# Weight rows 1088 bytes apart and activations in a high and a low block, in a two-layer encoder

## The chip, the cores and the metric

The kernel runs on one core of one Trainium2 chip. The metric is the time of one execution on the device in microseconds; less is better. A median of three runs is given for the kernel before.

## The reference

A two-layer encoder over 256 tokens and 16 learned meta tokens (272 rows), width 2048, all in float32. Each layer does this:

```python
h = rmsnorm(x)
q, k, v, f, ga, gf = split(h @ w_in)              # one input projection
attn = softmax(rope(norm(q)) @ rope(norm(k)).T / sqrt(128)) @ v   # 8 heads, 2 key/value heads
fr   = Re(fft2(f))                                # per group of 128 channels, over positions and channels
x = x + (sigmoid(ga) * (attn @ w_attn_br) + sigmoid(gf) * (fr @ w_four)) @ w_out
h2 = rmsnorm(x)
x = x + (silu(dwconv3(h2 @ w_up_gate)) * (h2 @ w_up_val)) @ w_down    # inner width 5632
```

The 16 meta rows are put in front before layer 0 and dropped at the end.

## The kernel before

Activations lie transposed in SBUF: channels over the 128 partitions, tokens along the free dimension. A projection takes a tile of 128 x 128 weights as the stationary operand and a tile of activations, 128 channels by all tokens, as the moving one.

To keep float32 accuracy with the `float32r` type, every operand is split into a high part and a low part, and a product is three matmuls: high weights by high activations, high weights by low activations, low weights by high activations (L357, L358, L359 in `group`). Where two tokens' halves fit one PSUM bank, the first two are one matmul of twice the width (L353).

Weights stream from HBM in chunks of 512 KB: 4 row tiles (`CW`) of 128 rows by 256 columns (`MG` = 2 column tiles). The list `order` holds all groups of chunks in the order in which they are used, and `chunks` is that list flattened. `load_raw` (L238) issues the transfer of a chunk into a ring of 4 buffers `raw`, and in some stages every third chunk into one of 2 more buffers `raw5`. `advance` (L254) keeps the transfers that far ahead of TensorE and puts splits on the list `todo`. `split_w` (L279) makes the high part `wh` on ScalarE (L286) and the low part `wl` on VectorE (L288), each in a ring of 3 buffers of 128 x 4 x 256 elements. `next_split` hands a pair to `group`. `fold_w` makes sums and differences of weight rows for the Fourier groups of layer 0 in the buffer `wpm`.

The normalised input of a layer's projections is `xHL`: for each of the 16 channel tiles the high part of 272 tokens and behind it the low part, so a tile takes 2176 bytes of a partition. `gHL` (inner activations of layer 0) has the same form. The high and low parts of the query and attention tiles (`q`, tags q1 and q2) and of the gated merge (`mH`, `mL`, in the tiles aH and aL) are separate tiles with 1088 bytes for each channel tile.

Layer 0 works on all 272 tokens. Layer 1 leaves the first 14 out in most projections (258 columns) and all 16 in the value half of its feed-forward part (2 x 256 columns).

The order of a layer: the Fourier inputs (`f`), `k`, `v`, `q`; then the mixing stage, two halves of the branch groups `ga`, `gf`, `s`, `a` in the order BRANCH_ORDER, each half followed by 8 groups `o` of the output projection; then the feed-forward part. In layer 0 this is `ug` and `uv` for 24 and then 20 inner tiles, each followed by 8 groups `d`. In layer 1 a fast scheme of block products is mixed in: `products` (L1402) multiplies activations by weights with the roles exchanged, so that the 128 x 128 activation tile (`opnd`, or a part of `xHL`) is stationary and 512 columns of weights move (L1419). At the end four groups `t` (tails, L1500) do the same for the inner tiles that are left. The generator `prepare` makes the sums of weights which these products need, on VectorE and with GpSimd's queue for its transfers, while layer 0's feed-forward part runs. Small work (attention, norms, Fourier steps) sits in generators in the list `shadow`, and `step` runs one piece of it after every second triple of matmuls.

TensorE's instructions run in program order. SBUF tiles come from pools: `per` (whole run), `wp` (weight buffers), and one pool for each stage, `mix0`, `ffn0`, `mix1`, `ffn1`.

Of the kernel before, what the change touches and what calls it, by code (L numbers as in the profile page):

```python
# [10 lines left out]
F32 = mybir.dt.float32  # L11
F32R = mybir.dt.float32r
# [4 lines left out]
P = 128  # L17
# [43 lines left out]
TAIL_ORDER = (2, 3, 0, 1)  # L61
F0 = 1536

def _branch(text):
# [91 lines left out]
def encoder_kernel(ctx, tc, xT, params, consts, bmat, cfold, csign, w_fl, w_f64c, w_in, w_abr, w_four, w_f64, w_out, w_up, w_down, w_vn, w_dn, w_dt, out):  # L156
# [53 lines left out]

    chunks, folded, mix, summed, stage, small_w = [], set(), {}, {}, {}, {}
    t, done = 0, 0
    for key, chs in order:
        for j, ch in enumerate(chs):
            n = 0
            if key[0] == 1 and key[1] in ("t", "ug", "uv"):
                n = due(t) - done
                t += 1
            if n:
                mix[key, j] = n  # L220
                for s, p, k in PRODUCTS[done:done + n]:
                    if p in (3, 4, 5, 6):
                        summed[len(chunks)] = (min(s, len(VSETS)), (3, 0, 1, 2)[p - 3], k)
                    chunks.append(pchunks[done])
                    done += 1
                first_mix = min(first_mix, len(chunks) - n) if done > n else len(chunks) - n
            if key[:2] == (0, "s"):
                folded.add(len(chunks))
            if key[1] in BRANCH:
                stage[len(chunks)] = key[0]  # L230
                if key[1] == "gf" and j == 0:
                    small_w[len(chunks) + KT // CW] = (key[0], key[2])
            chunks.append(ch)
    st = {"raw": 0, "fetch": 0, "next": 0, "grp": 0, "stage": None}
    raws, splits = {}, {}
    RAW, LOOK = 4, 2

    def load_raw(i):  # L238
        src, n = chunks[i]
        assert i not in summed or summed[i] in ready_sums  # L240
        if i in small_w:
            assert "r64" not in st
            st["r64"] = wp.tile([64, MG * P], F32, tag="r64", name="r64", bufs=1)
            nc.sync.dma_start(st["r64"], w_f64[small_w[i]])
        if (i >= first_mix if st["stage"] == DEPTH else stage.get(i, -1) == st["stage"]) and (i - first_mix) % 3 == 2:
            r = st["pool"].tile([P, CW, MG * P], F32, tag="raw5", name=f"raw{i}", bufs=2)
        else:
            r = wp.tile([P, CW, MG * P], F32, tag="raw", name=f"raw{i}", bufs=RAW)
        nc.sync.dma_start(r, src)
        raws[i] = r  # L250
# [3 lines left out]
    def advance(upto):  # L254
        while st["raw"] < min(upto + RAW + 2 * (upto > first_mix or stage.get(upto, -1) == st["stage"]), len(chunks)):
# [17 lines left out]
    def fold_w(i):  # L273
        r = wp.tile([P, CW, MG * P], F32, tag="wpm", name=f"wpm{i}", bufs=1)
        for o, op in ((0, ALU.add), (2, ALU.subtract)):
            nc.vector.tensor_tensor(r[:, o:o + 2], raws[i][:, 0:2], raws[i][:, 2:4], op=op)
        raws[i] = r

    def split_w(i, a, b, parts="hl"):  # L279
        if i not in splits:  # L280
            splits[i] = tuple(wp.tile([P, CW, MG * P], F32R, tag=t, name=f"{t}{i}") for t in ("wh", "wl"))
        h, lo = splits[i]
# [82 lines left out]
    def split_w64(l, i):  # L365
        r = st.pop("r64")
        w = wp.tile([96, MG * P], F32R, tag="w64", name="w64", bufs=2)
# [70 lines left out]
    XT = per.tile([P, KT, T], F32, name="XT")  # L438
    xf = per.tile([P, KT * 2 * T + 8], F32R, name="xHL")
    xHL = xf[:, :KT * 2 * T].rearrange("p (k r t) -> p k r t", k=KT, r=2)  # L440
    xH, xL = xHL[:, :, 0, :], xHL[:, :, 1, :]
    prm = per.tile([P, P_N], F32, name="prm")
# [57 lines left out]
    def norm_split(m, goff):  # L500
        gc = prm[:, goff + m:goff + m + 1]
        nc.scalar.activation(xH[:, m, :], XT[:, m, :], AF.Copy, scale=gc)
        nc.vector.scalar_tensor_tensor(xL[:, m, :], XT[:, m, :], gc, xH[:, m, :].bitcast(F32),
# [109 lines left out]
    for l in range(DEPTH):  # L613
        last = l == DEPTH - 1
        lo = 14 if last else 0
        lo2 = 16 if last else 0
        W, W2 = T - lo, T - lo2
        hold = {}

        with tc.tile_pool(name=f"mix{l}", bufs=1) as mp:  # L620
            E = mp.tile([P, 4, 2, TH] if last else [P, NG, T], F32, tag="q1b" if last else "q1", name="E")
            e64 = mp.tile([2 * NG, TH], F32, tag="u", name="e64", bufs=2) if last else None
            AHn = 3 * 4 * T
            ALn = 2 * 4 * T
            o1 = []
# [425 lines left out]
            def attention(kv, rq):  # L1051
# [8 lines left out]
                PH = PHf.rearrange("p (b h t) -> p b h t", b=3, h=4)  # L1060
                PL = PLf.rearrange("p (b h t) -> p b h t", b=2, h=4)

# [89 lines left out]
            for i in range(4):  # L1152
# [3 lines left out]
                if last:  # L1156
                    if i in (0, 2):
                        until(hold, "vt" if i == 0 else "fold")
                        for t_, n in ((qH, "q1"), (qL, "q2")):
                            t_.append(mp.tile([P, 4, T], F32R, tag=n + "ab"[i // 2], name=n))  # L1160
                elif i == 0:
                    until(hold, "vt")
                    until(hold, "fold")
                    for t_, n in ((qH, "q1"), (qL, "q2")):
                        t = mp.tile([P, NH, T], F32R, tag=n, name=n)
                        t_ += [t[:, 0:4], t[:, 4:8]]
# [25 lines left out]
            for half in range(2):  # L1192
                mH = mL = None
                for n_, (kind, i) in enumerate(BRANCH_ORDER[half]):
# [45 lines left out]
        with tc.tile_pool(name=f"ffn{l}", bufs=1) as fp:  # L1240
# [50 lines left out]
            if last:  # L1291
                X0, X1 = 26, 32
                XF = XT.rearrange("p k t -> p (k t)")
                asum = XF[:, 0:NQ * P].rearrange("p (k t) -> p k t", k=NQ)
                own = fp.tile([P, KS - (X1 - X0), SEQ], F32, name="act")
                lent = XF[:, NQ * P:NQ * P + (X1 - X0) * SEQ].rearrange("p (k t) -> p k t", t=SEQ)
# [145 lines left out]
                for i in UP_ORDER:  # L1442
# [136 lines left out]
```

## Time and profile before

| | us |
|---|---|
| median of 3 runs | 2527.54 (2526.27 to 2527.87) |
| the profiled execution | 2529.31 |
| its span in the profile | 2527.5 |
| TensorE busy (PE) | 2517.7 |
| weight loads busy (PEld) | 2436.3 |
| VectorE busy (DVE) | 1987.5 |
| ScalarE busy (ACT) | 1340.5 |
| GpSimd busy (POOL) | 203.9 |

The profile is of one execution. A matmul's duration in it is that of a pipelined instruction, which overlaps the next; how fast TensorE goes is read from the distance between starts, or from the count of matmuls in a stretch. PEld rows are weight loads: each matmul has one, and it runs beside the matmul before it. A row of the windows gives, for a stretch, each engine's busy time and its instruction count in brackets, the granted clock of TensorE (1.00 is full), the busy share of the DMA engines and what they moved in GB/s. Rows of the timeline give start, length, engine, line, operation and operands, written as output<-inputs; neighbours of one kind are merged and counted.

### The profile page before, as it was taken

To read this page: it belongs to the slowest core of one execution; us is meant where nothing else is said; L and a number is where in the kernel's file an instruction comes from. 1 tells how busy PE (TensorE), PEld (TensorE's weight loads), DVE (VectorE), ACT (ScalarE), POOL (GpSimd) and SP (SyncE) were. 2 spreads that over 40 slices of the span, in tenths; PEclk is the share of its full clock that TensorE was granted. 3 is DMA by queue.
4 is the path that set the end of the run, shared out by engine and by line. 5 is a ranking of instruction groups with operands and counts; after the bars stand their busy time and mean duration, and the time that the engine had idled before them with its cause. 6 is when DMAs were issued, how large, how long until landed. Compare 5 with 4: busy or idle time off the path is not lost.

```text
span 2527.5 us, 47924 instructions
## 1 busy us (share of the span) xinstructions
PE 2517.7 (100%) x18848; PEld 2436.3 (96%) x18848; DVE 1987.5 (79%) x3159; ACT 1340.5 (53%) x1913; POOL 203.9 (8%) x394
## 2 busy tenths in 40 slices
PE   9999999999999999999999999999999999999999
PEld 8999999999999999999999999999988899998887
DVE  7687866778878667888768877666878787898898
ACT  5455444554444334444445555444676665666665
POOL 0000000012212221222200000000000000000000
PEclk9999999999999999999999999999999999999999
DMA  7544558879999999999975647888888887788887
GB/s 248 167 155 157 190 190 249 260 247 371 394 324 387 391 378 380 378 383 386 390 280 195 201 154 232 270 256 261 255 262 290 299 290 236 261 280 288 279 302 269
DMA packets 194802, 706.85 MB, mean 280 GB/s; under 512 B 22144, under 2 KB 27392, under 8 KB 194320
## 3 DMA queue, kind: packets, MB, share of 16 engines
q1 hardware_dynamic: 146768, 517.09, 58.6%
q0 software_dynamic: 46368, 184.57, 21.2%
q8 instruction: 147, 2.41, 0.4%
q10 hardware_dynamic: 1440, 2.13, 0.2%
q14 instruction: 79, 0.65, 0.1%
HBM read 623.32 MB, written 111.15 MB: 291 GB/s over the span
## 4 chain that ended last, share of the span: by engine, by line
PE 99%; DVE 0%; DMA 0%; issue 0%; POOL 0%; ACT 0%; ACTq 0%; POOLq 0%
PE ps_p L1419 14%; PE ps_ug L359 7%; PE ps_ug L358 7%; PE ps_ug L357 7%; PE ps_d L358 4%; PE ps_uv L358 4%; PE ps_d L357 3%; PE ps_uv L359 3%; PE ps_d L359 3%; PE ps_uv L357 3%; PE ps_o L358 2%; PE ps_ga L358 2%; PE ps_gf L358 2%; PE ps_o L357 2%; PE ps_ga L359 2%; PE ps_o L359 2%
## 5 line engine op out<-in xcount | busy, mean ns | idle before, releaser
L286 ACT CAST wh<-raw 128x1024 fp32r<-128x1024 f32 (+1 forms) x961 | 999.9, 1045 | 913.4 <-PE ps_ug L358 214.5
L288 DVE TENSOR_TENSOR wl<-raw,wh 128x1024 fp32r<-128x1024 f32 (+1 forms) x961 | 1158.4, 1216 | 410.2 <-ACT wh L286 399.3
L358 PE MATMUL ps_ug<-xHL,wh 128*128 128x272 f32 (+1 forms) x1408 | 401.5, 285 | 0.0
L357 PE MATMUL ps_ug<-xHL,wh 128*128 128x272 f32 (+1 forms) x1408 | 400.8, 285 | 0.0
L359 PE MATMUL ps_ug<-xHL,wl 128*128 128x272 f32 (+1 forms) x1408 | 400.5, 286 | 0.1
L358 PEld LDWEIGHTS ps_ug<-xHL,wh 128*128 128x128 f32 x1408 | 264.7, 188 | 3.2
L357 PEld LDWEIGHTS ps_ug<-xHL,wh 128*128 128x128 f32 x1408 | 264.6, 188 | 3.3
L359 PEld LDWEIGHTS ps_ug<-xHL,wl 128*128 128x128 f32 x1408 | 264.1, 188 | 1.2 <-DVE wl L288 0.8
L1419 PE MATMUL ps_p<-wh,opnd 128*128 128x512 f32 x816 | 222.7, 393 | 0.0
L358 PE MATMUL ps_uv<-xHL,wh 128*128 128x272 f32 x704 | 203.3, 289 | 0.0
L358 PE MATMUL ps_d<-gHL,wh 128*128 128x272 f32 x704 | 202.9, 288 | 0.0
L357 PE MATMUL ps_d<-gHL,wh 128*128 128x272 f32 x704 | 202.9, 288 | 0.0
L359 PE MATMUL ps_uv<-xHL,wl 128*128 128x272 f32 x704 | 202.6, 288 | 0.0
L357 PE MATMUL ps_uv<-xHL,wh 128*128 128x272 f32 x704 | 202.3, 287 | 0.0
L359 PE MATMUL ps_d<-gHL,wl 128*128 128x272 f32 x704 | 202.1, 287 | 0.0
L1419 PEld LDWEIGHTS ps_p<-wh,opnd 128*128 128x128 f32 x816 | 148.4, 188 | 29.4 <-ACT wh L286 0.2
L357 PE MATMUL ps_ga<-xHL,wh 128*128 128x272 f32 (+1 forms) x512 | 147.8, 289 | 0.0
L519 DVE TENSOR_TENSOR wi<-wi,wi 128x512 f32<-128x512 f32 x224 | 146.8, 684 | 0.0
L357 PE MATMUL ps_gf<-xHL,wh 128*128 128x272 f32 (+1 forms) x512 | 146.8, 287 | 0.0
L358 PE MATMUL ps_o<-mL,wh 128*128 128x272 f32 (+1 forms) x512 | 146.5, 286 | 0.0
L358 PE MATMUL ps_ga<-xHL,wh 128*128 128x272 f32 (+1 forms) x512 | 146.1, 285 | 0.0
L359 PE MATMUL ps_o<-mH,wl 128*128 128x272 f32 (+1 forms) x512 | 146.1, 285 | 0.0
(380 smaller groups left out, 5969.4 us busy)
## 6 DMA issues: line engine op xcount, KB each, us to landing
raw<-in_w_up SPq DMA_DIRECT2D x288, 512.0 KB, 6.3
raw<-in_w_in SPq DMA_DIRECT2D x191, 512.0 KB, 3.8
raw<-in_w_down SPq DMA_DIRECT2D x88, 512.0 KB, 7.0
wi<-in_w_dn POOLq DMA_DIRECT2D x80, 512.0 KB, 9.7
ft<-wi POOLq DMA_DIRECT2D x80, 512.0 KB, 7.9
raw<-ft SPq DMA_DIRECT2D x80, 512.0 KB, 4.6
raw<-in_w_out SPq DMA_DIRECT2D x64, 512.0 KB, 4.2
raw<-fv SPq DMA_DIRECT2D x64, 512.0 KB, 4.8
```

What stands on the lines that cost most here:

```text
L286: nc.scalar.copy(h[:, a:b], r[:, a:b])
L288: nc.vector.tensor_tensor(lo[:, a:b], r[:, a:b], h[:, a:b].bitcast(F32), op=ALU.subtract)
L357: nc.tensor.matmul(o, h[:, c, sl], a, start=kt == 0, stop=False)
L358: nc.tensor.matmul(o, h[:, c, sl], b, start=False, stop=False)
L359: nc.tensor.matmul(o, lo[:, c, sl], a, start=False, stop=kt == nk - 1)
L519: tt = lambda *v, **kw: tc.keep_in_program_order(nc.vector.tensor_tensor(*v, **kw))
L1419: nc.tensor.matmul(ps[h], x, w[:, 512 * h:512 * h + 512], start=fresh and (s_, q) in BEGIN and first, stop=(s_, q) in END and end, skip_gr ...
```

## The change

The split weights `wh` and `wl` become flat buffers of 4 x 272 elements; a row tile's 256 columns take the first 256 of each 272, so row tiles lie 1088 bytes apart, as far as the activation tiles of 272 tokens. Chunks that serve as the moving operand (the products and the tails, the set `streamed`) stay dense, 1024 bytes apart, in the same buffers. `xHL` and `gHL` are laid out as one block of all high parts and one of all low parts. The starts of `xHL` (one for each layer), `gHL`, the query tiles, `mH`, `mL` and `opnd` are moved by fixed numbers of elements, and `act` gets 48 unused elements behind it, which moves what lies behind. To make room, the small weight buffers `r64`, `w64` and `wpm` go from the pool `wp` to the stage's pool, and in layer 0's mixing stage one extra buffer `raw5` is kept instead of two, so the transfers run five chunks ahead there instead of six.

```diff
+CS = T
+X_PAD, X_AT = 64, (28, 60)
+G_AT = 12
+M_AT = ((60, 60), (22, 22))
+Q_AT = (((12,), (20,)), ((62, 46), (62, 62)))
+A_PAD, O_AT = 48, 16
...
+                    streamed.add(len(chunks))
                     chunks.append(pchunks[done])
...
+            if key[:2] == (1, "t"):
+                streamed.add(len(chunks))
...
+    def extra(i):
+        if st["stage"] == DEPTH:
+            return 2 * (i >= first_mix)
+        return 0 if st["stage"] is None or stage.get(i, -1) != st["stage"] else 1 + st["stage"]
...
-        if (i >= first_mix if st["stage"] == DEPTH else stage.get(i, -1) == st["stage"]) and (i - first_mix) % 3 == 2:
-            r = st["pool"].tile([P, CW, MG * P], F32, tag="raw5", name=f"raw{i}", bufs=2)
+        more = extra(i)
+        if more and (i - first_mix) % (2 + 3 // more) == 1 + 3 // more:
+            r = st["pool"].tile([P, CW, MG * P], F32, tag="raw5", name=f"raw{i}", bufs=more)
...
+    def weight_rows(w, dense):
+        if dense:
+            return w[:, :CW * MG * P].rearrange("p (c m) -> p c m", c=CW)
+        return w.rearrange("p (c m) -> p c m", c=CW)[:, :, :MG * P]
...
-            splits[i] = tuple(wp.tile([P, CW, MG * P], F32R, tag=t, name=f"{t}{i}") for t in ("wh", "wl"))
+            splits[i] = tuple(weight_rows(wp.tile([P, CW * CS], F32R, tag=t, name=f"{t}{i}"), i in streamed) for t in ("wh", "wl"))
...
-    xf = per.tile([P, KT * 2 * T + 8], F32R, name="xHL")
-    xHL = xf[:, :KT * 2 * T].rearrange("p (k r t) -> p k r t", k=KT, r=2)
-    xH, xL = xHL[:, :, 0, :], xHL[:, :, 1, :]
+    xf = per.tile([P, KT * 2 * T + X_PAD], F32R, name="xHL")
+    xHLs = [xf[:, o:o + KT * 2 * T].rearrange("p (r k t) -> p r k t", r=2, k=KT) for o in X_AT]
+    xHL, xH, xL = xHLs[0], xHLs[0][:, 0], xHLs[0][:, 1]
...
-            ALn = 2 * 4 * T
+            ALn = 2 * 4 * T + M_AT[l][1]
...
-                            t_.append(mp.tile([P, 4, T], F32R, tag=n + "ab"[i // 2], name=n))
+                            o = Q_AT[l][t_ is qL][i // 2]
+                            t = mp.tile([P, 4 * T + o], F32R, tag=n + "ab"[i // 2], name=n)
+                            t_.append(t[:, o:o + 4 * T].rearrange("p (h t) -> p h t", t=T))
...
-                            mH = mHf[:, :8 * T].rearrange("p (k t) -> p k t", k=8)
-                            mL = mLf[:, :8 * T].rearrange("p (k t) -> p k t", k=8)
+                            mH = mHf[:, M_AT[l][0]:M_AT[l][0] + 8 * T].rearrange("p (k t) -> p k t", k=8)
+                            mL = mLf[:, M_AT[l][1]:M_AT[l][1] + 8 * T].rearrange("p (k t) -> p k t", k=8)
...
-                gHL = fp.tile([P, FF_SPLIT[0], 2, T], F32R, tag="gHL", name="gHL")
-                gH, gL = gHL[:, :, 0, :], gHL[:, :, 1, :]
+                gf = fp.tile([P, FF_SPLIT[0] * 2 * T + G_AT], F32R, tag="gHL", name="gHL")
+                gH, gL = (gf[:, G_AT + FF_SPLIT[0] * T * r:G_AT + FF_SPLIT[0] * T * (r + 1)].rearrange("p (k t) -> p k t", t=T) for r in range(2))
...
-                own = fp.tile([P, KS - (X1 - X0), SEQ], F32, name="act")
+                own = fp.tile([P, (KS - (X1 - X0)) * SEQ + A_PAD], F32, name="act")
...
-                    t_ = fp.tile([P, 2, 3, P], F32R, tag="opnd", name="opnd", bufs=2)
+                    t_ = fp.tile([P, 6 * P + 64], F32R, tag="opnd", name="opnd", bufs=2)
+                    t_ = t_[:, O_AT:O_AT + 6 * P].rearrange("p (r n t) -> p r n t", r=2, n=3)
...
-                        ps = group((l, "uv", i), lambda kt: (xHL[:, kt, :, lo2:T],), W2)
+                        ps = group((l, "uv", i), lambda kt: (xHL[:, :, kt, lo2:T],), W2)
```

More of the change, by code (lines that the diff above doesn't have):

```diff
@@ L209, in due @@
         return d0 + (d1 - d0) * (t - t0) // (t1 - t0)
-    chunks, folded, mix, summed, stage, small_w = [], set(), {}, {}, {}, {}
+    chunks, folded, streamed, mix, summed, stage, small_w = [], set(), set(), {}, {}, {}, {}
     t, done = 0, 0
@@ L242, in load_raw @@
             assert "r64" not in st
-            st["r64"] = wp.tile([64, MG * P], F32, tag="r64", name="r64", bufs=1)
+            st["r64"] = st["pool"].tile([64, MG * P], F32, tag="r64", name="r64", bufs=1)
             nc.sync.dma_start(st["r64"], w_f64[small_w[i]])
-        if (i >= first_mix if st["stage"] == DEPTH else stage.get(i, -1) == st["stage"]) and (i - first_mix) % 3 == 2:
-            r = st["pool"].tile([P, CW, MG * P], F32, tag="raw5", name=f"raw{i}", bufs=2)
+        more = extra(i)
+        if more and (i - first_mix) % (2 + 3 // more) == 1 + 3 // more:
+            r = st["pool"].tile([P, CW, MG * P], F32, tag="raw5", name=f"raw{i}", bufs=more)
         else:
@@ L254, in advance @@
     def advance(upto):
-        while st["raw"] < min(upto + RAW + 2 * (upto > first_mix or stage.get(upto, -1) == st["stage"]), len(chunks)):
+        while st["raw"] < min(upto + RAW + extra(upto), len(chunks)):
             load_raw(st["raw"])
@@ L273, in fold_w @@
     def fold_w(i):
-        r = wp.tile([P, CW, MG * P], F32, tag="wpm", name=f"wpm{i}", bufs=1)
+        r = st["pool"].tile([P, CW, MG * P], F32, tag="wpm", name=f"wpm{i}", bufs=1)
         for o, op in ((0, ALU.add), (2, ALU.subtract)):
@@ L366, in split_w64 @@
         r = st.pop("r64")
-        w = wp.tile([96, MG * P], F32R, tag="w64", name="w64", bufs=2)
+        w = st["pool"].tile([96, MG * P], F32R, tag="w64", name="w64", bufs=2)
         nc.scalar.copy(w[0:64], r)
@@ L501, in norm_split @@
         gc = prm[:, goff + m:goff + m + 1]
+        xH, xL = (xHLs[goff // KT % DEPTH][:, r] for r in range(2))
         nc.scalar.activation(xH[:, m, :], XT[:, m, :], AF.Copy, scale=gc)
@@ L617, in encoder_kernel @@
         W, W2 = T - lo, T - lo2
+        xHL, xH, xL = xHLs[l], xHLs[l][:, 0], xHLs[l][:, 1]
         hold = {}
@@ L1060, in attention @@
                 PH = PHf.rearrange("p (b h t) -> p b h t", b=3, h=4)
-                PL = PLf.rearrange("p (b h t) -> p b h t", b=2, h=4)
+                PL = PLf[:, :2 * 4 * T].rearrange("p (b h t) -> p b h t", b=2, h=4)
                 def scores(item):
@@ L1164, in encoder_kernel @@
                     for t_, n in ((qH, "q1"), (qL, "q2")):
-                        t = mp.tile([P, NH, T], F32R, tag=n, name=n)
+                        o = Q_AT[l][t_ is qL][0]
+                        t = mp.tile([P, NH * T + o], F32R, tag=n, name=n)[:, o:o + NH * T].rearrange("p (h t) -> p h t", t=T)
                         t_ += [t[:, 0:4], t[:, 4:8]]
@@ L1294, in encoder_kernel @@
                 asum = XF[:, 0:NQ * P].rearrange("p (k t) -> p k t", k=NQ)
-                own = fp.tile([P, KS - (X1 - X0), SEQ], F32, name="act")
+                own = fp.tile([P, (KS - (X1 - X0)) * SEQ + A_PAD], F32, name="act")
+                own = own[:, :(KS - (X1 - X0)) * SEQ].rearrange("p (k t) -> p k t", t=SEQ)
                 lent = XF[:, NQ * P:NQ * P + (X1 - X0) * SEQ].rearrange("p (k t) -> p k t", t=SEQ)
```

## The prediction

> **What bounds the kernel now.** I read the page's busy times and its chain first, then the groups, then the windows, then the timeline of TensorE.
>
> ```profile
> span 2527.5 us, 47924 instructions
> PE 2517.7 (100%) x18848; PEld 2436.3 (96%) x18848; DVE 1987.5 (79%) x3159; ACT 1340.5 (53%) x1913; POOL 203.9 (8%) x394
> PE 99%; DVE 0%; DMA 0%; issue 0%; POOL 0%; ACT 0%; ACTq 0%; POOLq 0%
> L286 ACT CAST wh<-raw 128x1024 fp32r<-128x1024 f32 (+1 forms) x961 | 999.9, 1045 | 913.4 <-PE ps_ug L358 214.5
> L288 DVE TENSOR_TENSOR wl<-raw,wh 128x1024 fp32r<-128x1024 f32 (+1 forms) x961 | 1158.4, 1216 | 410.2 <-ACT wh L286 399.3
> L358 PE MATMUL ps_ug<-xHL,wh 128*128 128x272 f32 (+1 forms) x1408 | 401.5, 285 | 0.0
> ```
>
> TensorE never waits: the chain is 99% matmuls, and L358 has 0.0 us of idle time before 1408 of them. ScalarE, which makes the high part of every weight (L286), idles 913 us, most of it until TensorE gives a buffer back. So only the spacing of the matmuls matters. The 285 ns of a matmul is a pipelined duration; the spacing comes from counts in stretches that hold almost only one width:
>
> ```profile
> core 0: us, PE busy (x) PEld busy (x) DVE busy (x) ACT busy (x) POOL busy (x), PEclk, DMA share, GB/s
> 541.00:1334.00 793.00, 793.00 (x6326) 792.92 (x6325) 620.95 (x950) 342.78 (x431) 154.35 (x293) 1.00 0.97 367
> 1603.50:1666.50 63.00, 63.00 (x527) 63.00 (x527) 38.61 (x53) 25.07 (x29) 3.54 (x8) 1.00 0.78 247
> ```
>
> The first stretch is layer 0's feed-forward part, 272 columns: 793.0 / 6326 = 125.4 ns a matmul. The second is layer 1's output projection, 258 columns: 63.0 / 527 = 119.5 ns. PEclk is 1.00, so no throttle explains either. Whether that is the least these widths can take is seen where the same code goes at two speeds, in the products at L1419, 512 columns wide. The timeline of TensorE, start and merged length:
>
> ```profile
> 2005.41 1.10 PE L1419 MATMUL ps_p<-wh,xHL 128*128 128x512 f32 x4
> 2006.34 0.63 PE L1419 MATMUL ps_p<-wl,xHL 128*128 128x512 f32 x2
> 2006.80 1.10 PE L1419 MATMUL ps_p<-wh,xHL 128*128 128x512 f32 x4
> 2007.74 0.62 PE L1419 MATMUL ps_p<-wl,xHL 128*128 128x512 f32 x2
> 2008.20 0.28 PE L357 MATMUL ps_ug<-xHL,wh 128*128 128x258 f32 x1
> ...
> 2514.09 1.07 PE L1419 MATMUL ps_p<-wh,opnd 128*128 128x512 f32 x4
> 2514.99 0.61 PE L1419 MATMUL ps_p<-wl,opnd 128*128 128x512 f32 x2
> 2515.45 1.07 PE L1419 MATMUL ps_p<-wh,opnd 128*128 128x512 f32 x4
> 2516.36 0.61 PE L1419 MATMUL ps_p<-wl,opnd 128*128 128x512 f32 x2
> 2516.81 1.07 PE L1419 MATMUL ps_p<-wh,opnd 128*128 128x512 f32 x4
> 2517.72 0.61 PE L1419 MATMUL ps_p<-wl,opnd 128*128 128x512 f32 x2
> 2518.17 0.63 PE L1500 MATMUL ps_t<-wh,t 128*128 128x512 f32 x2
> ```
>
> With xHL as the stationary operand, 12 matmuls take 2008.20 - 2005.41 = 2.79 us, 232.5 ns each. With opnd, 18 take 4.08 us, 226.7 ns each: 5.8 ns less, with no operation changed. What differs is where the operands lie. As the kernel's memory is allotted, wh starts at byte 94,368 of a partition in buffers 4096 apart, and the two opnd buffers at 222,112 and 225,184 with tiles 512 apart: each such moving operand starts a multiple of 256 bytes from its stationary one. xHL starts at 25,728 with tiles 2176 apart and a low part 1088 further, so modulo 256 the distance alternates among 32, 96, 160 and 224. I take from this that TensorE reads two operands at once, the moving one of a matmul and the weights of the next, and that a distance that stays put lets them settle into a pattern without collisions.
>
> **The change part by part.** (1) Weight rows of 1088 bytes. In the groups at L357 to L359 before, activations advance 1088 or 2176 bytes a tile and weights 1024, so the distance walks. After, both advance 1088, a weight buffer is 4 x 1088 = 4352 = 17 x 256 bytes, the halves of a row lie 512 apart, wl follows wh by 13,056 = 51 x 256, and the low block of xHL its high one by 17,408 = 68 x 256. I added up the tile sizes of after: wh moves to 94,592, the layers' pools start at 127,168, and the activation's start minus the weight's, modulo 256, is 112 for xHL, gHL, q and m of layer 0 (272 columns), 40 for xHL and 48 for q and m at 258 columns, 48 for the 512-column value groups (L353), 0 as before for opnd, and 0 instead of 64 for the tails (L1500). Only layer 1's k and v (240) and the folded groups fall outside, and where a row ends one load in six lies 64 bytes off.
>
> The gain per matmul has no row of its own at these distances, so I bound it. At best every width runs at the settled products' rate, 226.7 / 512 = 0.443 ns a column: 120.4 ns at 272 (4.9 ns less), 114.2 at 258 (5.3 less). The loop bounds give 9792 matmuls of 272 columns (68 groups of 96 for f, k, v, q, ga, gf, ug and uv, 1152 for a and o, 2112 for d) and 5184 of 258 (42 groups of 96 and 1152): 9792 x 4.9 = 48 us and 5184 x 5.3 = 27 us. L353's 192 and the tails' 84 give at most 276 x 5.8 = 2 us. At worst the constant distance is a bad one and the excess doubles: +75 us. For 272 I take the settled value, since it is the same machine with the same pair of reads, less 4 us for runs that must settle anew after attention and rope work is put between groups. For 258 I take half, because the weight load itself comes near the spacing there:
>
> ```profile
> 442.28 0.34 PE L391 MATMUL ps_s<-fr,wh 128*128 128x276 f32 x1
> 442.46 0.23 PE L392 MATMUL ps_s<-fr,wl 128*128 128x138 f32 x1
> 442.52 0.34 PE L391 MATMUL ps_s<-fr,wh 128*128 128x276 f32 x1
> ...
> 442.76 0.34 PE L391 MATMUL ps_s<-fr,wh 128*128 128x276 f32 x1
> ```
>
> These pairs stream 414 columns, 183 ns at 0.443, but start 240 ns apart: 120 ns for each of the two weight loads. If a load keeps that pace beside a stream, 119.5 ns at 258 columns is already its bound; if the collisions make it so, it falls with them. Also, the 2112 such matmuls of layer 1's ug come in runs of 24 between products and settle anew each time.
>
> (2) Transfers. A faster TensorE asks for weights sooner, and one stretch has no room:
>
> ```profile
> 160.00:380.00 220.00, 220.00 (x1769) 220.00 (x1768) 164.17 (x307) 106.44 (x173) 3.48 (x3) 1.00 0.51 174
> 770.00:970.00 200.00, 200.00 (x1597) 200.00 (x1596) 144.97 (x190) 74.98 (x81) 41.80 (x79) 1.00 1.00 384
> 970.00:1270.00 300.00, 300.00 (x2396) 300.00 (x2396) 243.57 (x360) 133.49 (x173) 63.00 (x120) 1.00 1.00 381
> ACT wh L286 <- DMA raw<-in_w_up: 7.0, 3, 2.8
> GB/s 248 167 155 157 190 190 249 260 247 371 394 324 387 391 378 380 378 383 386 390 280 195 201 154 232 270 256 261 255 262 290 299 290 236 261 280 288 279 302 269
> ```
>
> From 770 to 1270 us the engines of the DMA are busy throughout at about 382 GB/s, since the weight sums of the side task travel too. Only 3 waits for raw (7 us, from 600 to 1270) show. The fastest slice of the span moves 394 GB/s; at that rate those 500 us shrink to 485, where the matmuls alone (3993 x 4.9) would allow 480. So 5 us of the gain go back to waiting.
>
> (3) Buffers. Layer 0's mixing stage keeps one extra raw buffer instead of two, five ahead instead of six. Its transfers fill half the time (0.51 at 160 to 380 us), so I cost it at nothing; without that cover each late load would cost up to the 2.8 us of the longest wait above. The small weight tiles move to the stage's pool with their counts unchanged: nothing.
>
> (4) Split instructions. L286 and L288 now write four rows of 256 with gaps. Between nothing and some 30 ns each (the short pieces cost a start, not a second pass); ScalarE's 913 us of idle time, and the three weight buffers before TensorE, hide it: nothing. No wait is added.
>
> Sum: 48 - 4 + 13 + 2 - 5 = 54 us. The profiled execution took 2529.3 us (span 2527.5), so 2475; the median of the runs is 1.8 us lower, 2473.
>
> The Trainium skill, "SBUF — State Buffer", section "Who interferes with whom", gives TensorE two independent read ports, one for the moving operand and one for weight loads, and says that TensorE never waits on anyone. By that the sum would be 0. The two timings of L1419 speak against it, 226.7 and 232.5 ns for the same instructions.
>
> **The rivals.** *Nothing settles.* The rule above, or a pattern that 272 columns do not have: 512 columns are 8 x 256 bytes, so a settled product ends where it began, while 272 columns end 64 bytes on. For it: in o the distance stays for six matmuls at a time already, and its matmuls are no shorter than those of ug (285 above):
>
> ```profile
> L357 PE MATMUL ps_o<-mH,wh 128*128 128x272 f32 x256 | 73.5, 287 | 0.0
> ```
>
> Then only the tails' and L353's 2 us come: 2526.
>
> *The transfers or weight loads take over.* The matmuls could go at 120, but raw lands late in the stretch at 1.00, and 258 columns stay at 119.5. Then layer 0's feed-forward gives half of 6326 x 4.9 = 31 us, 258 gives nothing, and the rest of layer 0 (3466 x 4.9) 17 us: 15 + 17 - 4 = 28 us, 2500. For it: 1.00 in the windows and 120 ns in the pairs; against it: only 7 us of waits for raw now.
>
> *Slower: the constant distance is a bad one.* Now good and bad distances alternate and average 125.4. If 112 bytes is a distance at which every load meets the stream, the long unbroken runs are worst, since nothing shakes them out: layer 0's 6326 feed-forward matmuls at twice the excess (130.3) cost 31 us, 2559. It decides from a spacing above 125.4 at 272. Against it: different starts for 272 and 258 columns, and 0 kept for 512, where 0 is measured as the good one. For it: no row shows 112.
>
> **How the numbers follow.** The forecast, TensorE settling in most of the work, has 0.61; the takeover 0.18; nothing settles 0.07; slower 0.14. Likeliest: 2473, its own range 2450 (all 75 + 2 us) to 2492 (272 alone, less the 4 and 5, with a few us of slow splits). Range: 2448 to 2530, the upper end taking in the takeover and no change and leaving out the slower case. A measurement of this kernel tells about 0.2% (5 us) from no change. Faster 0.79, same 0.07, slower 0.14.
>
> **What would show it.** Right: over 793 us' worth of feed-forward work, 6326 matmuls in about 760 to 768 us; timeline rows of ps_ug at 0.12 us in a row without 0.13; L1419 with opnd unchanged at 226.7; tails near 227 instead of 233; the windows from 770 on at 1.00 and a little over 382 GB/s, with more waits of L286 for raw. The takeover shows as idle time before PEld at L357 in that stretch. Wrong: 272 columns at 125 or above, or 258 columns moving while 272 do not; or idle time of TensorE in layer 0's mixing stage, which I priced at nothing.

## The result, and the profile after

The changed kernel takes 2519.2 us (median of 6 runs, 2514.9 to 2520.2); the kernel before took 2527.4 beside it (6 runs, 2526.3 to 2529.6). The ratio is 0.9965, with a 95% interval of 0.9952 to 0.9978: 8 us faster, where 54 were forecast. The profiled execution took 2520.2 us. One execution of a later run, e_dense, took 5614.9 us with the matmuls of layer 0's feed-forward part 316 ns apart, for a reason that stays open, and its median is that of the other ten.

The page of the changed kernel, busy times, chain and the costliest groups:

```profile
span 2518.4 us, 47932 instructions
PE 2503.5 (99%) x18848; PEld 2423.2 (96%) x18848; DVE 1988.6 (79%) x3159; ACT 1339.9 (53%) x1913; POOL 203.9 (8%) x394
PE 44%; DVE 1%; issue 0%; ACT 0%; DVEq 0%; ACTq 0%
L306 ACT CAST wh<-raw 128x1024 fp32r<-128x1024 f32 (+1 forms) x961 | 998.6, 1044 | 888.9 <-PE ps_ug L378 190.2
L308 DVE TENSOR_TENSOR wl<-raw,wh 128x1024 fp32r<-128x1024 f32 (+1 forms) x961 | 1159.2, 1218 | 391.0 <-ACT wh L306 378.1
L378 PE MATMUL ps_ug<-xHL,wh 128*128 128x272 f32 (+1 forms) x1408 | 399.1, 284 | 0.0
```

TensorE is busy for 2503.5 us of 2518.4; before it was 2517.7 of 2527.5. So its busy time shrank by 14 us, and some 5 us of new idle time stand against that. The chain was followed back only as far as a wait at 1369 us, so its 44% is nearly all of the span behind that point. The split instructions cost what they did (1044 and 1218 ns, before 1045 and 1216). The same stretches as in the prediction, by the windows of the changed kernel:

```profile
core 0: us, PE busy (x) PEld busy (x) DVE busy (x) ACT busy (x) POOL busy (x), PEclk, DMA share, GB/s
541.00:1334.00 793.00, 792.63 (x6395) 792.32 (x6394) 629.04 (x969) 347.00 (x440) 153.06 (x291) 1.00 0.97 368
1603.50:1666.50 63.00, 63.00 (x533) 63.00 (x532) 38.21 (x53) 25.60 (x29) 3.55 (x8) 1.00 0.81 249
160.00:380.00 220.00, 220.00 (x1780) 220.00 (x1779) 166.21 (x307) 107.37 (x175) 3.20 (x3) 1.00 0.52 178
770.00:970.00 200.00, 200.00 (x1617) 200.00 (x1616) 145.56 (x190) 75.80 (x82) 43.22 (x82) 1.00 1.01 389
```

In 793 us fit 6395 matmuls instead of 6326: 124.0 ns instead of 125.4 at 272 columns, not 120.4. At 258 columns it is 63.0 / 533 = 118.2 instead of 119.5. The stretch of heavy transfers moves 389 GB/s and TensorE still does not wait there, nor in layer 0's mixing stage.

What was given back shows in the waits of TensorE. Before the change:

```profile
PE ps_f L424 <- ACT wh L286: 5.7, 3, 4.5
PE ps_uv L354 <- DVE wl L288: 0.3, 1, 0.3
```

After it (engine, line, what it waited for: us in total, times, longest):

```profile
PE ps_f L444 <- ACT wh L306: 4.8, 2, 4.5
PE ps_pv L1142 <- DVE PL L1134: 2.9, 3, 1.8
PE ps_f L873 <- DVE wl L308: 2.7, 1, 2.7
PE ps_ss L943 <- DVE sqm L972: 0.4, 1, 0.4
PE ps_uv L374 <- DVE wl L308: 0.3, 1, 0.3
```

Three lines are new, all in layer 1's mixing stage: `ps_pv` is attention's product of probabilities and values, `ps_f` at L873 belongs to the Fourier steps, `ps_ss` to the norms. The longer waits also lower the clock behind them, as windows of the changed kernel behind the 2.7 and the 1.8 us show:

```profile
1366.00:1370.00 4.00, 1.28 (x12) 1.06 (x9) 3.33 (x6) 0.65 (x1) 0.00 (x0) 0.99 0.03 10
1370.00:1377.00 7.00, 7.00 (x35) 6.83 (x35) 5.52 (x9) 3.68 (x6) 0.00 (x0) 0.52 0.66 226
1463.00:1467.00 4.00, 4.00 (x26) 4.00 (x25) 2.01 (x6) 1.76 (x4) 0.00 (x0) 0.69 0.40 141
```

After the 2.7 us wait PEclk is 0.52 for 7 us, which by 7 x 0.48 loses 3.4 us more; by this estimate the wait costs more than twice its length. Two questions were left: why 124 and not 120, and where the waits come from.

### The profile page after: what moved, and what is told of

It reads as the page before. It is cut to its first block, busy times and chain, and to the rows that moved or that the text cites. A ratio compares the mean times of both kernels' runs of the same rounds, so it can differ in the third digit from the quotient of the medians.

```text
span 2518.4 us, 47932 instructions
## 1 busy us (share of the span) xinstructions
PE 2503.5 (99%) x18848; PEld 2423.2 (96%) x18848; DVE 1988.6 (79%) x3159; ACT 1339.9 (53%) x1913; POOL 203.9 (8%) x394
## 5 line engine op out<-in xcount | busy, mean ns | idle before, releaser
L306 ACT CAST wh<-raw 128x1024 fp32r<-128x1024 f32 (+1 forms) x961 | 998.6, 1044 | 888.9 <-PE ps_ug L378 190.2
L308 DVE TENSOR_TENSOR wl<-raw,wh 128x1024 fp32r<-128x1024 f32 (+1 forms) x961 | 1159.2, 1218 | 391.0 <-ACT wh L306 378.1
L379 PE MATMUL ps_ga<-xHL,wl 128*128 128x272 f32 (+1 forms) x512 | 146.2, 286 | 0.0
```

The lines of the kernel that those rows point to most:

```text
L306: nc.scalar.copy(h[:, a:b], r[:, a:b])
L308: nc.vector.tensor_tensor(lo[:, a:b], r[:, a:b], h[:, a:b].bitcast(F32), op=ALU.subtract)
L379: nc.tensor.matmul(o, lo[:, c, sl], a, start=False, stop=kt == nk - 1)
```

## The experiments

The theories were these. *Spacing*: the fixed distance shortens the matmuls, but by less than thought; its rival is that the addresses do nothing. *Waits*: the small weight tiles, which I had costed at nothing, or attention's padded tile make them; the rival is that TensorE simply arrives in layer 1 too soon for the other engines.

**e_dense and e_dense2: only the weight rows undone.** All engines issue the same instructions in the same order as in the changed kernel.

```diff
     def weight_rows(w, dense):
+        dense = True
         if dense:
```

> The changed kernel with one edit: the weight rows are packed at 1024 bytes again inside their 4352-byte buffers, so the distance walks by 64 bytes a row; the activations, buffers and the order of all instructions stay as after the change. If the gain of the change comes from the fixed distance: the spacing at 272 columns goes from 123.9 back to 125.4 ns and at 258 from 119.2 to about 120, and the time is about 15 us above that of the changed kernel (2534), so slower than before the change, because layer 1's stalls stay. If it comes from anything else (high and low blocks, buffers): spacing unchanged and 2519.

> The kernel of e_dense once more, for its profile: the spacing at 272 columns back at 125.0 to 125.5 ns and at 258 at 119.7 to 120.5 if the fixed distance made the gain, and unchanged (123.7 and 119.2) if not; the waits of ps_pv for PL stay, since nothing of their cause is undone; 2527 to 2530 us.

Measured: 2528.8 us beside 2527.2 of before, ratio 1.0006 (0.9997 to 1.0015). Undoing the row pitch of the weights alone costs 9.6 us against the changed kernel, all of the gain and some more, though not the 15 us expected. The profile is that of e_dense2 (one run, 2527.6 us); its window of layer 0's feed-forward part, then its waits of TensorE:

```profile
541.00:1334.00 793.00, 793.00 (x6342) 792.96 (x6341) 621.95 (x954) 343.66 (x432) 153.48 (x291) 1.00 0.98 368
PE ps_pv L1143 <- DVE PL L1135: 2.8, 3, 1.7
PE ps_f L874 <- DVE wl L309: 1.4, 1, 1.4
```

793.0 / 6342 = 125.0 ns. Of the 1.4 ns between 125.4 and 124.0 the fixed distance thus brought 1.0, and what e_dense keeps of the change (blocks, starts, buffers) 0.4. The waits for PL stay as they were although TensorE reaches layer 1 later here (its first 258-column matmul starts at 1348.9 us, in the changed kernel at 1339.7): something in the new code makes them, not its early arrival. The wait for wl stays too, but at 1.4 us instead of 2.7.

**p_grid: the spacing by itself.**

```diff
+for n in WIDTHS:
+    for a in STEPS + (None,):
+        ...
+        hi, low = X[:, at:at + n], X[:, at + 512:at + 512 + n]
+        ...
+        nc.tensor.matmul(t, W[:, 0, c, sl], hi, ...)
+        nc.tensor.matmul(t, W[:, 0, c, sl], low, ...)
+        nc.tensor.matmul(t, W[:, 1, c, sl], hi, ...)
```

> This kernel computes nothing of the encoder: TensorE alone runs triples (high weights with high operand, high weights with low operand, low weights with high operand) from one resident weight tile, 48 matmuls for each of six widths (256, 258, 272, 304, 384, 512) and each of 11 fixed distances modulo 256 bytes (0 to 224 by 32, and 40, 48, 112), and once for each width with a distance that walks by 64 bytes a row. My first theory (collisions that a fixed distance avoids, with a cost that goes by columns): 226.7 ns at 512 and 120.4 at 272 at distance 0, and the walking case slower than the best fixed one by some 5 ns. Rival 1 (the cost above N/2.4 is one of each matmul and not of each column): 10 to 14 ns above N/2.4 at every width, so 272 settles at 123 to 127 whatever the distance, 258 at 118 to 121. Rival 2 (two reads that never meet): all distances and the walk agree within 1 ns at each width.

Measured, ns from start to start over the last 35 of the 48 matmuls, worked out from the starts in its trace (272: second pass; 304 columns and the distances 40 and 48 left out):

```
width  distance 0     32     64     96    112    128    160    192    224   walk
256        120.00 117.77 117.74 120.11 113.34 118.66 118.66 117.77 118.29 117.00
258        120.00 119.89 118.66 119.91 118.66 122.23 119.97 120.83 120.00 121.37
272        125.51 125.71 126.60 125.34 123.29 126.63 123.54 123.31 126.66 124.97
384        173.34 173.34 173.34 176.71 173.29 176.00 173.34 174.69 173.31 174.14
512        226.69 233.29 228.80 233.40 231.29 233.46 234.29 233.40 233.40 232.29
```

No other engine works here, so the differences along a row are TensorE's own, and rival 2 falls. My first theory falls with the 125.5 at 272; rival 1 is right on the size at 272 and about right at 258 (up to 122.2), but not on "whatever the distance". The addresses are not all, though: in a first pass over 272 columns 96 and 224 bytes gave 126.6 and 125.3, the other way round. p_state below takes that up. Distance 0 at 512 gives the 226.7 ns of the opnd products to the decimal. But the same distance gives 125.5 at 272, which is no better than the walk. At distance 0 three entries lie on one line: 120.0, 173.3 and 226.7 are 53.3 ns apart for 128 columns, 0.4167 ns a column with 13.3 ns on top. So there the excess belongs to each matmul and not to its columns; at 272 columns it is 12.2. At other distances it changes with the width as well, from 6.7 ns (256 columns at 112) to 21 (512 at 160). The best of the tried distances at 272 leaves 10.0, 123.3 ns; the walk has 11.6. That is the whole prize here: 1.7 ns.

**s1: other distances in the kernel.**

```diff
-X_PAD, X_AT = 64, (28, 60)
-G_AT = 12
-M_AT = ((60, 60), (22, 22))
+X_PAD, X_AT = 64, (0, 2)
+G_AT = 0
+M_AT = ((0, 0), (0, 0))
+M_PAD = 60, 22
...
-            ALn = 2 * 4 * T + M_AT[l][1]
+            ALn = 2 * 4 * T + M_PAD[l]
```

> The changed kernel with other offsets of the activations only: the distances modulo 256 become 0 for xHL and 64 for gHL and 128 for m in layer 0 (272 columns, before 112), 64 for xHL and 216 for m in layer 1 (258 columns, before 40 and 48); order and buffers unchanged. Theory that the distance sets the settled spacing and 0 is the good one, as for opnd: ug and uv of layer 0 at 120 to 122 ns, d and o apart from them, total about 2500. Rival, any fixed distance does the same: 123.7 for all three and 2519 in total. Rival, 112 was chosen since others are worse: ug at 126 to 130, total 2535 to 2560.

Measured: 2537.6 us (one run), 10 us slower than before. The window of its feed-forward part:

```profile
541.00:1334.00 793.00, 793.00 (x6312) 792.92 (x6311) 619.47 (x948) 343.07 (x430) 154.26 (x293) 1.00 0.97 367
```

793 / 6312 is 125.6 ns, behind the 125.0 of e_dense2's walk. All 272-column matmuls take 1310.2 us by their starts, before 1310.0, so these distances win nothing; the 10 us are the waits, which stay, and slower 258-column matmuls (638.1 us, before 632.2). A fixed distance is a gain only where the distance is a good one; my reading of opnd, that 0 is good, holds here for 512 columns and not for 272. The rival "slower" of the prediction had this at 112; there the changed kernel has 123.9 ns, and only e_rows, below, 125.8.

**p_real: the changed kernel's addresses, TensorE alone.** What it has other than p_grid: rows of 1088 bytes for weights and activations, and a group's real order of chunks.

> This kernel computes nothing of the encoder: TensorE alone runs groups of 96 matmuls from resident operands with the addresses of the changed kernel (weights and activations 1088 bytes a row, high and low blocks, the last chunk of a group sorted by column tile), at 272 and 258 columns and as the value groups of layer 1 (512 and 256 columns in turn), for 20 distances modulo 256 bytes. By p_grid: at 272 columns 112, 160 and 192 are the good ones at 123.3 to 124 ns, 0 and 32 at 125.6, 64 and 96 to 128 at 126 to 127; the same as in the changed kernel (123.7 at 112) and in s1 (125.8 at 0). If waits or contention of the full kernel set its spacing and not the addresses, TensorE alone is faster at the same distance, 121 or less. At 258, 64 and 112 about 118.7, 40 at 119, 128 and 192 at 121 to 122.

Measured, mean ns of a group's matmuls from the 13th on (starts in its trace):

```
272: 112 and 176 123.9 | 16 124.5 | 48 and 192 124.6 | 240 124.7 | 80 125.0 | 144 125.1 | 96 125.4 |
     160 125.5 | 32 and 64 125.6 | 128 125.7 | 0 and 208 125.8 | 40 126.1 | 232 126.3 | 56 126.7 | 224 127.0 | 72 127.7
258: 48 118.4 | 240 118.8 | 72 and 144 118.9 | 112 119.0 | 40 119.1 | ... | 128 120.9 | 16 121.3 | 96 121.8
```

112 gives 123.9 ns and 0 gives 125.8, without any other engine; the kernel's spacings are 123.9 (e_pl, below) and 125.6 (s1). So no wait or contention of the full kernel has to be called in for 124 instead of 120. The change had picked the best distances of this table, 112 at 272 and 48 at 258 (a and o; ug at 40). It is not a table of distances alone: 160, expected among the good ones by p_grid (123.5), has 125.5 here.

**e_small: the small weight tiles back in the weight pool.**

```diff
-            st["r64"] = st["pool"].tile([64, MG * P], F32, tag="r64", name="r64", bufs=1)
+            st["r64"] = wp.tile([64, MG * P], F32, tag="r64", name="r64", bufs=1)
...
-        w = st["pool"].tile([96, MG * P], F32R, tag="w64", name="w64", bufs=2)
+        w = wp.tile([96, MG * P], F32R, tag="w64", name="w64", bufs=2)
```

> The changed kernel with one edit: the small weight tiles r64 and w64 are taken from the weight pool again, as before the change, and not from the stage's pool; all distances stay as after the change. If the stalls at layer 1's start (about 11 us between 1330 and 1575 us) come from the small tiles' loads and splits having moved there from layer 0, they go: TensorE's windows from 1330 to 1380 full again, the rope's wait for its transfer under 0.5 us, and 2508 to 2511 us. If the stalls come from TensorE reaching layer 1 sooner, or from attention's order alone: 2517 to 2520.

Measured: 2514.6 us, ratio to before 0.9955 (0.9941 to 0.9969). The times of the two kernels overlap (2513.2 to 2520.9 us here, 2514.9 to 2520.2 for the changed one), so it is the trace that shows the effect: the wait of ps_f for wl is gone. Where it came from can be followed in the timelines. Before, SP loaded the small tiles for layer 1's first three gates during layer 0:

```profile
414.74 0.47 SPq L244 DMA_DIRECT2D r<-in_w_f  x1
448.82 0.48 SPq L244 DMA_DIRECT2D r<-in_w_f  x1
482.95 0.48 SPq L244 DMA_DIRECT2D r<-in_w_f  x1
```

After the change the buffers belong to the stage's pool and exist only once layer 1 has begun (SP, VectorE and TensorE of the changed kernel):

```profile
1319.09 0.48 SPq L258 DMA_DIRECT2D r<-in_w_f  x1
1326.23 0.47 SPq L258 DMA_DIRECT2D r<-in_w_f  x1
1334.01 0.47 SPq L258 DMA_DIRECT2D r<-in_w_f  x1
...
1354.04 4.31 SPq L264 DMA_DIRECT2D raw<-fw  x2
1358.45 2.56 SPq L949 DMA_DIRECT2D qs<-qp  x4
...
1364.62 0.73 DVE L953 TENSOR_TENSOR qs<-qs,cst 128x544 f32<-128x544 f32 x1 [2.84 <-DMA qs<-qp]
...
1369.41 0.93 PE L873 MATMUL ps_f<-hA,wl 128*128 128x138 f32 x5 [2.72 <-DVE wl L308]
```

Their splits now fall into VectorE's work at layer 1's start, and the order there shifts. A raw load is stuck in SP's queue until 1358.0, the swap transfers for the rope sit behind it, VectorE waits 2.84 us for them, and the wl that TensorE needs next is queued behind that. In the kernel before, the rope's wait was 0.38 us:

```profile
1376.45 0.72 DVE L931 TENSOR_TENSOR qs<-qs,cst 128x544 f32<-128x544 f32 x1 [0.38 <-DMA qs<-qp]
```

The order of VectorE's and ScalarE's instructions at layer 1's start in e_small is that of before again, and its waits of TensorE are:

```profile
PE ps_f L444 <- ACT wh L306: 5.9, 2, 4.9
PE ps_pv L1142 <- DVE PL L1134: 2.6, 3, 1.8
PE ps_uv L374 <- DVE wl L308: 0.3, 1, 0.3
```

The waits of ps_pv are untouched, so 2508 was not reached: a second cause.

**e_pl: and attention's tile at its exact size.**

```diff
-                PLf = mp.tile([P, ALn], F32R, tag="aL", name="PL")
+                PLf = mp.tile([P, 2 * 4 * T], F32R, tag="aL", name="PL")
...
-                PL = PLf[:, :2 * 4 * T].rearrange("p (b h t) -> p b h t", b=2, h=4)
+                PL = PLf.rearrange("p (b h t) -> p b h t", b=2, h=4)
```

> The small weight tiles from the weight pool again, as in e_small (2514.6 us), and one more edit: attention's tile PL is allotted at its exact size, as before the change, and not as the first part of a tile with 88 bytes of padding. TensorE's own instruction order is then the one before the change again, the seven products of ps_pv in one piece. Theory: with the padded tile the fifth product of each ps_pv is tied to VectorE's write of PL for the next head; without it the three waits of ps_pv for PL (2.6 us, 1.8 the longest) and the lower clock behind them are gone, 1450 to 1540 us shows no idle TensorE, and the time is 4 to 6 us lower, 2509 to 2511. Rival: the wait only moves to another place of attention, since TensorE is early there and VectorE is not: 2514 to 2515.

Measured: 2508.5 us, ratio 0.9936 (0.9924 to 0.9948), 18 us faster than before. Five of its six runs took 2507.6 to 2509.2 us and one 2518.3, to which p_state below comes back. Its waits of TensorE:

```profile
PE ps_f L444 <- ACT wh L306: 4.8, 2, 4.5
PE ps_uv L374 <- DVE wl L308: 0.3, 1, 0.3
```

In the changed kernel TensorE's timeline has the seven products of one ps_pv in two pieces:

```profile
1457.55 0.29 PE L1141 MATMUL ps_pv<-PH,VH 128*128 128x258 f32 x1
...
1458.77 0.28 PE L377 MATMUL ps_ga<-xHL,wh 128*128 128x258 f32 x1
1460.85 0.39 PE L1142 MATMUL ps_pv<-PL,VH 128*128 128x258 f32 x1 [1.79 <-DVE PL L1134]
```

In e_pl the same product follows at once:

```profile
1460.72 0.28 PE L1141 MATMUL ps_pv<-PH,VH 128*128 128x258 f32 x1
1460.84 0.28 PE L1142 MATMUL ps_pv<-PL,VH 128*128 128x258 f32 x1
```

The PL that the fifth product waits for is the one made from the transposes just before it, by the code the next head's. No data ties the two, and the exact size removes the tie. That the compiler, seeing a part of a larger tile, takes the reads and writes for overlapping ranges is my reading, which no run shows. It can't be all: in layer 0 the same tile has 240 bytes of padding, and there the seven products stay in one piece in the changed kernel too (150.2 to 150.9 us).

**e_plonly: the fourth corner.** The edit of e_pl on the changed kernel, without that of e_small.

> The changed kernel with one edit: PL at its exact size, small weight tiles still in the stage's pool. With e_small (2514.6) and e_pl (2508.5) this closes the square. If the two causes add: TensorE's waits of ps_pv for PL gone, the wait of ps_f for wl (2.7 us) still there, and 2513 us. If one stall only hides the other: 2517 to 2519.

Measured: 2512.9 us, ratio 0.9945 (0.9931 to 0.9958); ps_f still waits 1.4 us for wl. Against before in the same runs the four corners are -8.2 us (changed), -12.6 (small tiles), -13.9 (PL) and -18.1 (both). The causes add, 4.4 and 5.7 to 9.9, as far as these numbers tell: each has an interval of some 3 us either way.

**e_x62: 8 bytes further.**

```diff
-X_PAD, X_AT = 64, (28, 60)
+X_PAD, X_AT = 64, (28, 62)
```

> e_pl (2508.5) with the activations of layer 1 8 bytes further: distance 48 instead of 40 at 258 columns for xHL, and 56 instead of 48 for the value groups; order unchanged. From the table of p_real: 258 columns 118.36 instead of 119.13 over 4032 matmuls, 3.1 us less; the value groups 179.5 instead of 175.2 a matmul over 384, 1.7 us more: 2507 in all. If the table of TensorE alone does not hold in the kernel: 2508.5 or above, with ug at 119 as now.

Measured: 2508.1 us, ratio 0.9928 (0.9915 to 0.9942), not told apart from e_pl. By the starts in the traces all 258-column matmuls take 627.4 us instead of 628.2, a gain of 0.8 and not 3.1; the value groups' 512-column matmuls went from 231.4 to 235.5 ns (four longer gaps left out), about as p_real had it. p_real's difference of 0.8 ns between 40 and 48 did not carry over.

**e_rows: the last chunk not sorted.**

In every group the matmuls of the last chunk run one column tile after the other, so that the group's first accumulator is complete early. This edit to e_pl leaves that out.

```diff
-            if j == len(chs) - 1:
-                cm.sort(key=lambda v: v[1])
```

> e_pl (2508.5) with the last chunk of a group no longer sorted by column tile: only one load in six, not one in three, then lies 64 bytes off. By p_real the last chunk of a group takes 124.7 ns a matmul at 272 columns and the others 123.6: 2448 matmuls x 1.1 = 2.7 us less from spacing. Against it: a group's first accumulator is complete 12 matmuls (1.5 us) later, so VectorE and ScalarE take it up later and some groups wait. Without new waits 2505.5 to 2506.5; with them 2509 or above.

Measured: 2521.7 us (10 runs), ratio 0.9968 (0.9953 to 0.9982): 13 us behind e_pl. One wait of 1.4 us, of ps_f for wl, is back, though the small tiles are loaded early here, so other shifts of the order can bring it too. Most of the rest is spacing: the 272-column matmuls take 10.4 us more. The windows of its feed-forward part and of 200 us of layer 0's mixing stage:

```profile
541.00:1334.00 793.00, 793.00 (x6305) 793.00 (x6304) 618.40 (x949) 339.68 (x427) 153.19 (x290) 1.00 0.97 366
300.00:500.00 200.00, 200.00 (x1626) 200.00 (x1625) 140.94 (x222) 93.02 (x132) 8.30 (x18) 1.00 0.75 234
```

And e_pl's:

```profile
541.00:1334.00 793.00, 793.00 (x6400) 792.92 (x6399) 628.04 (x968) 346.85 (x439) 154.05 (x291) 1.00 0.97 369
300.00:500.00 200.00, 200.00 (x1620) 200.00 (x1619) 141.08 (x220) 92.02 (x132) 8.27 (x18) 1.00 0.75 234
```

The 200 us of the mixing stage are a little faster without the sort (1626 matmuls instead of 1620), as expected. The feed-forward part, with the same addresses and instructions of the same kind, is at 125.8 to 125.9 ns from its second group to its last, where e_pl has 123.9. Three of the ten runs took 2508.2 to 2510.4 us, the other seven 2520.5 to 2525.3.

**p_state: one distance, two spacings.** p_real's addresses, each group behind one matmul of another width:

```diff
+for v in SHAKE:
+    nc.tensor.matmul(ps[0][:, :v], W[0][0][:, 0, :P], X[:, 0:v], start=True, stop=True)
+    ...
```

> This kernel computes nothing of the encoder: TensorE alone runs groups of 192 matmuls of 272 columns with the addresses of the changed kernel, each group behind one matmul of another width (260 to 500 by 16), so that it starts 16 times in a different phase; four cases: distance 112 with one chunk of a group sorted by column tile as in the changed kernel, and 112, 176 and 16 with no sorted chunk. In e_rows (112, no sorted chunk) the feed-forward part ran at 125.8 ns and the mixing part at 123.6, with the same addresses. Theory: at one distance there are two settled spacings and the phase at the start picks one: of the 16 groups at 112 unsorted some stay at 123.6 and some at 125.8 to the end; with the sorted chunk all end at 123.6. Rival: the 125.8 of e_rows comes from other work of its feed-forward part (transfers, VectorE), and TensorE alone settles at 123.6 in all 16 groups.

The groups were of 144 matmuls, not 192 as the expectation has it. Measured, from the starts in the trace, groups by the spacing of their second and third chunk of 24:

```
112, one chunk sorted: 12 groups at 123.6, 4 at 125.8 (behind 292, 468, 484 and 500 columns)
112, none sorted:      12 groups at 123.6, 4 at 125.8 (behind the same four widths)
176: 13 groups at 124.7, 2 at 126.4 to 126.8, 1 at 123.6
16:  16 groups at 124.0 to 124.6
```

The theory of settled spacings held, with three of them at 176: the width of the matmul in front of the group decides, at 112 by the same four widths each time, and the group then keeps its spacing through 144 matmuls. That the sorted chunk brings all groups to 123.6 did not: four stay at 125.8 around it. Two windows of 14 us in the unsorted case at 112, one behind 276 columns and one behind 292 (each count holds two matmuls that reach over the edges):

```profile
322.00:336.00 14.00, 14.00 (x115) 14.00 (x115) 0.00 (x0) 0.00 (x0) 0.00 (x0) 1.00 0.01 1
340.00:354.00 14.00, 14.00 (x113) 14.00 (x112) 0.00 (x0) 0.00 (x0) 0.00 (x0) 1.00 0.00 1
```

So 125.8 ns at distance 112 is a spacing of TensorE's own, and a feed-forward part that begins in the wrong phase (the expectation's word for how the group's start falls) and stays there explains e_rows. That its three short runs began in the good phase, and e_pl's run of 2518.3 us in the bad one, fits, but no profile of these was taken. The median of e_rows is therefore no verdict on the sorting, and runs of this one kernel lie up to 17 us apart (2508.2 to 2525.3).

## Why the prediction was wrong

*The direction and its reason were right.* Time is set by the spacing of TensorE's matmuls, and the spacing depends on the operands' distance (e_dense, p_grid). Why it does is not shown: that two reads collide was a reading of two timings, and it remains one. "Settling" is no mark of the constant distance either: ug and uv of the changed kernel take 123.9 ns in group after group, and those of the kernel before, whose distance walks, 125.3 as steadily.

*"For 272 I take the settled value": the step that failed.* I carried 226.7 ns over as 0.443 ns a column. p_grid shows a cost of each matmul that depends on width and distance together, 13.3 ns for 512 at 0 and 10.0 for 272 at 112. By the row of distance 0 the carrying over fails even at 256 columns: 0.443 ns a column would be 113.3 ns, and 120.0 was measured. So 4.9 ns a matmul became 1.5, and "48 - 4" became 15.8 us: all 272-column matmuls take 1310.0 us before and 1294.2 after, by their starts. My doubt in "nothing settles", that 272 columns are no multiple of 256 bytes, was not the reason: 256 columns are four times 256 bytes, and there the step fails too.

*258 columns, 13 us:* 632.2 us before, 628.2 in e_pl where no wait disturbs, so 4. The same step: half of a gain that was itself too large.

*Value groups and tails, 2 us:* all 512-column matmuls went from 414.1 to 412.2 us in e_pl, 1.9, but that was luck. The tails gave 0.4 us, at 227.9 ns instead of 233.0, as forecast, and the value groups 0.2, at 233.2 instead of 234.0 with their few longer gaps counted. The other 1.3 came from the products, which the sum did not count.

*Transfers, 5 us given back:* nothing was given back, since 124 ns asks for less than I feared (389 GB/s, no wait of TensorE). *Raw buffers and split instructions, nothing:* right. The bound of 30 ns for a split, and the start that each short piece was to cost, stood on no row; the splits took 1 ns less and 2 ns more than before.

*"The small weight tiles move to the stage's pool with their counts unchanged: nothing":* wrong by 4.4 us. I counted buffers and not from when they exist: a tile of a stage's pool was not filled before the stage. The loads moved from 415 to 483 us to 1319 to 1334 us, and I did not follow what they then met there.

*"No wait is added":* wrong by 5.7 us. A padded tile, read through a part of it, added one on TensorE itself. The diff showed the line and I did not cost it.

Together, by e_pl's and before's traces: 15.8 + 4.0 + 1.9 = 21.7 us, which is the difference of their spans (2527.5 and 2505.8). Of that the waits and the lower clock behind them took 12.6 us in the profiled executions (spans of 2518.4 and 2505.8), which leaves 9.1, and 9.9 of 18.1 in the medians, which leaves 8.2.

The Trainium skill, "SBUF — State Buffer", section "Who interferes with whom", calls TensorE's two read ports independent, by which the sum was 0. That does not hold here: e_dense differs from the changed kernel in addresses alone, and takes 9.6 us more. The Trainium skill, "TensorE: Matmul & The Clock Gate", section "Back-to-back issue gap", puts 2.5 ns on top of an isolated matmul's columns, and gives 131 ns at 512 columns for a stream of weight loads and matmuls. In p_grid, with a weight load beside each matmul, 512 columns took 226.7 to 234.3 ns, and the excess was 6.7 to 21 ns over all widths.

## What to carry to other kernels

When a timing of one shape is to be used for another, ask whether it goes by columns or by matmul; two widths at one distance would have told. TensorE alone, run with the kernel's addresses for 1 ms, gave a table that the kernel followed at 272 columns, while a difference of 0.8 ns at 258 did not carry over. Start such a run several times behind different matmuls, since one distance can have several spacings. After a change of layout compare the order of instructions and each engine's waits with those of before: here a pool and 88 bytes of padding gave back half of what the addresses had won. With these two edits undone the version takes 2508.5 us and beats both kernels.

## What the hardware did that I had not expected

A matmul of 256 columns goes from 113.3 ns at distance 112 to 120.1 at 96, with no other engine at work.

One set of addresses has more than one settled spacing, 123.6 and 125.8 ns at 272 columns and distance 112. The matmul in front picked one in p_state, and in e_rows one lasted for some 6200 matmuls. Distance 16 had no bad phase among 16 starts, at 124.0 to 124.6; the full kernel was not run at it.

A wait of 1.8 us was enough to lower the granted clock behind it to 0.69 over 4 us, and one of 2.7 us to 0.52 over 7. The Trainium skill, "TensorE: Matmul & The Clock Gate", section "What's actually happening", gives an idle window of about 3.4 us for the fall to half rate; here it fell after shorter waits.
